# Attention tiles, bias and carry taken and released head by head; a pair's units by head; the gate's projection first and v's last; the last super-block's v by TensorE

## The chip, the cores and the metric

One core of a Trainium2 chip. TensorE (PE, with its weight loads PEld) multiplies, VectorE (DVE), ScalarE (ACT) and GpSimd (POOL) work on tiles, SyncE (SP) issues nearly all DMAs. The metric is the device time of the program in microseconds. Before the change it is 1274.22, the median of three runs (1273.27 to 1274.51).

## The reference

One layer over 2048 prompt frames and 64 frames of a running stream (sample). The input projection has eight parts of 512 columns: q, k, v and gate of attention, and q, f, i and gate of the recurrence.

```python
aq, ak, av, ag, hq, hf, hi, hg = jnp.split(rms_norm(x, ln_g) @ w_in, SPLITS, axis=-1)
o_a = attn_fn(heads(aq), k, v).reshape(B, T, W_A) * jax.nn.silu(ag)
o_b, S = hgrn2_branch(hq, hf, hi, hg, lb, norm_g, s0)
y = x + jnp.concatenate([o_a, o_b], axis=-1) @ w_out
```

Attention has 8 heads of 64; a chunk of 64 frames attends to itself and the 8 chunks before, with a learned bias by distance. The recurrence has 4 heads of 128. Results are y after a last RMSNorm, the k and v rows of the last 512 prompt frames and of the sample, and the recurrence's states. All is float32; the kernel splits each operand in a high and a low part (xh, xl; w's two halves) and adds three products.

## The kernel before

The tokens are cut in four super-blocks of 512 (the second, super-block 1, has the 64 sample frames too: 576, in two blocks of 256 and 320). In each, 32 projection jobs run: four groups of eight, the hgrn jobs hf, hq, hi, hg of one head and the attention jobs pv, pq, pk, pg of one pair of heads. A job is 24 matmuls of one block into an accumulator (acc, two buffers), and an eviction: `ev_q`, `ev_k`, `ev_v`, `ev_g`. The first two and the last two jobs of a super-block run by halves of 256 tokens, in turn. The list JOBS gives the order; in the last super-block its end is written out by hand.

The order on all engines is written by a planner (`Plan`). Each activity is a generator; it yields a time or a condition, and is resumed on the planner's own clock. Tokens (`Tok`) stand for buffers: vT (3 buffers for evicted q, k, v, i), sig (2), tr (2 PSUM banks for transposes), pv, s_ps (one score buffer), ph (2), pr (4), mixa (2), sga (2, the gate of a pair), kv (the tiles kd, v and q of one pair), bias. On the chip each engine then runs its instructions in this order and waits for semaphores.

A pair opens when the kv token is free, that is when the pair before has ended its last PV unit: `open_` loads the carried k and v of the 512 tokens before (L713, L714) and the bias (L674). q, k and v wait in vT buffers till then. `ev_q` copies q of both heads into the tile (ACT L732) and makes the low part and the swapped half (DVE L736, L737). `ev_k` does the same for k (L749 from the accumulator, L756, L760); rows that leave the kernel are turned by 32x32 blocks on DVE (L771) and written by four DMAs (L777). `ev_v` must put tokens on partitions: it turns blocks on DVE (L632), writes them to DRAM in four DMAs (way, L652), reads them back (L656), and then splits them (ACT L620, DVE L624); rows that leave are written at L612. hi, the input of the recurrence, goes the same way (copy at L1211).

The attention of a pair has four units, (first 256 queries, head 0), (first, head 1), (second, head 0), (second, head 1); `softmax_rows` makes the scores of 128 queries (s, L858 adds the bias and finds the minimum, L875 exp, L879 scales), `p_group` transposes the probabilities (tr, L887, L890), `attend` multiplies with v (pv) and adds the parts (mixa, L925, L929). After head 1 of a unit's queries the gate is multiplied in (L1027) and the result goes to DRAM (mixd, L1032). `sample_a` does the sample's attention in super-block 1.

After the last job comes the output projection, seven products for each of eight token groups (`out_step`): rows come from mixd into slots (L1619), weights from wod (L1961) into tiles that have become free: w, b11, xh and xl, then kd, q and ql when the last scores are done, and ph and v after the last PV. Projection weights of super-blocks 1 to 3 come from wd (L437). All DMAs named here are issued by SP in one order.

All matmuls are recorded at L249 (the helper `mm`), all transposes at L253.

Of the kernel before, what the change touches and what calls it, by code (L numbers as in the profile page):

```python
# [8 lines left out]
F32 = mybir.dt.float32  # L9
# [37 lines left out]
JOBS = [[(k, g) for g in range(4) for k in ("hf", "hq", "hi", "hg", "pv", "pq", "pk", "pg")] for _ in SUPER]  # L47
# [136 lines left out]
def hymba_step(  # L184
# [67 lines left out]
    def transpose(out, x, idn):  # L252
# [4 lines left out]
                                     w=WBUFS, raw=RAWB, xn=XNB, kv=1, q=1, rec=1, sga=2, bias=1, gf=1, gi=1, gg=1,  # L257
# [349 lines left out]
    def rows_out(src, out, row, nt, cols, t):  # L607

        rows = src.shape[0]
        s4 = src.rearrange("p (a t j) -> p t a j", a=4, t=nt)  # L610
        for i in range(nt):
            sp.dma_start(out[row + i * P : row + i * P + rows, cols].rearrange("p (a j) -> p a j", a=4), s4[:, i])  # L612
        return C.dma(nt * rows)

    def split_rows(src, v, t0, nt, rows, t):
        s = src.rearrange("p (h a t j) -> p h a t j", h=2, a=2, t=nt)
        hi = v[:rows, t0 : t0 + nt, 0::3, :].rearrange("p t h (a j) -> p h a t j", a=2)
        lo = v[:rows, t0 : t0 + nt, 1:3, :].rearrange("p t h (a j) -> p h a t j", a=2)
        for h in range(2):
            act.copy(hi[:, h], s[:, h])  # L620
        t = C.act(nt * P + 150, t)
        yield "D", t
        for h in range(2):
            dve.tensor_sub(lo[:, h], s[:, h], f32(hi[:, h]))  # L624
        return C.dve(nt * P + 60, t)
# [44 lines left out]
    def load_bias(sb, p, d):  # L670
        yield from tk["bias"].get()
        nb = d.bias = T(wk, [P, 2, 640], F32, "bias", bufs=1)
# [16 lines left out]
        d.bias_at = t  # L689
        yield t  # L690
        sp.dma_start(biasd[p], nb)
        C.dma(655)

    def pair_jobs(sb, p):
# [6 lines left out]
        d.q_n = d.k_n = d.v_n = 0  # L701
        d.q_t = d.k_t = d.v_t = 0.0
        d.bias_at = d.cache = None

        def open_():

            yield from tk["kv"].get()
            d.kd = T(pa, [P, 2, WIN + NMAX], F32R, "kd")
            d.v = T(pa, [P, 9, 4, 64], F32R, "v")
            d.q = T(pa, [P, 2, QW], F32R, "q")  # L710
            if sb:
                cd = carry[sb - 1][p]
                sp.dma_start(f32(d.kd[:, :, 0:512]), cd[:, 0:2, :])  # L713
                sp.dma_start(f32(d.v[:, 0:4].rearrange("p t s d -> p (t s d)")),  # L714
                             cd[:, 2:4, :].rearrange("p a c -> p (a c)"))
                d.k_t = d.v_t = C.dma(1024)
            C.spawn(load_bias(sb, p, d), 1)
            if smp:
                C.spawn(sample_cache(d), 1)

        def ev_q(acc, off, bn, t):
# [7 lines left out]
            yield lambda: d.q is not None  # L729
            yield "A", t  # L730
# [3 lines left out]
            yield "D", t - 600.0  # L734
            for h in range(2):
                dve.tensor_sub(ql[own[h], h, c], st[own[h], :bn], f32(d.q[own[h], h, c]))  # L736
                dve.tensor_copy(d.q[own[1 - h], h, c], f32(d.q[own[h], h, c]))  # L737
                t = C.dve(1.8 * bn, t)
                if h == 0:
                    yield "D", t - 300.0  # L740
            tk["vT"].put(1, t)
            d.q_n += bn
            d.q_t = max(d.q_t, t)

        def ev_k(acc, off, bn, t):
# [6 lines left out]
            yield lambda: d.kd is not None  # L752
            yield "A", t
            c = slice(512 + off, 512 + off + bn)
            for h in range(2):
                act.copy(d.kd[own[h], h, c], kn[own[h], :bn])  # L756
                t = C.act(bn, t)
            yield "D", t - 600.0
            for h in range(2):
                dve.tensor_sub(d.kd[own[1 - h], h, c], kn[own[h], :bn], f32(d.kd[own[h], h, c]))  # L760
                t = C.dve(1.2 * bn, t)
            d.k_n += bn
            d.k_t = max(d.k_t, t)
            full = bn // P * P
            for c, w, out in ((0, full, nk_prompt if last else None), (full, bn - full, nk_sample)):
                if not w or out is None:
                    continue
                yield from tk["sig"].get()
                yield "D", t
                st = T(wk, [P, 512], F32, "sig", bufs=2)  # L770
                dve.transpose(st[:, :w], kn[:, c : c + w])  # L771
                t = C.dve(w, t)
                yield t
                row = 0 if c else off
                to = out[row : row + w, p * P : (p + 1) * P].rearrange("(n i) (a j) -> a i n j", i=32, a=4)
                for a in range(4):
                    sp.dma_start(to[a], st[32 * a : 32 * a + 32, :w].rearrange("p (n j) -> p n j", j=32))  # L777
                tk["sig"].put(1, C.dma(w))
            tk["vT"].put(1, t)
            yield from got_all(True)  # L780

        def ev_v(acc, off, bn, t):
# [6 lines left out]
            yield lambda: d.v is not None  # L789
            yield "A", t  # L790
            full = bn // P * P
            for c, w, rows, out in ((0, full, P, nv_prompt if last else None),
                                    (full, P if bn > full else 0, bn - full, nv_sample)):
                if not w:
                    continue
                t = yield from split_rows(vt[:rows, c : c + w], d.v, 4 + (off + c) // P, w // P, rows, t)
                if out is not None:
                    t = rows_out(vt[:rows, c : c + w], out, 0 if c else off, w // P, slice(p * P, (p + 1) * P), t)
            tk["vT"].put(1, t)
            d.v_n += bn  # L800
            d.v_t = max(d.v_t, C.now + 1000.0)
            yield from got_all(False)

        def got_all(k):
            if last and p == NPAIR - 1 and d.v_n == d.k_n == d.q_n == n:
                have.add("projected")
            if not last and (d.k_n if k else d.v_n) == n:
                yield (d.k_t if k else d.v_t) + 500.0
# [3 lines left out]
                else:  # L812
                    sp.dma_start(cd[:, 2:4, :].rearrange("p a c -> p (a c)"),
                                 f32(d.v[:, 4:8].rearrange("p t s d -> p (t s d)")))
# [18 lines left out]
        C.spawn(open_(), 1)  # L833
# [6 lines left out]
        return d, dict(g=ev_g, q=ev_q, k=ev_k, v=ev_v)  # L840

    def softmax_rows(d, h, qc, spans, bcol, nk, out):

        yield lambda: d.q_n >= qc + P and d.k_n >= qc + P and d.bias_at is not None
        yield max(d.q_t, d.k_t, d.bias_at) + 300.0
# [18 lines left out]
        d.left -= 1  # L864
        if d.left == 0:
            if d.sb == len(SUPER) - 1 and d.p == NPAIR - 1:
                have.add("scores")
                tk["x4"].put()
            tk["bias"].put()
# [13 lines left out]
    def vcols(v, t, h, rows):  # L883
        return v[:rows, t, 2 * h : 2 * h + 2, :].rearrange("p s d -> p (s d)")
# [48 lines left out]
    def attend(d, g0, h, prs, mixes, before, mine):  # L933
# [39 lines left out]
        yield lambda: d.v_n >= g0 + 256  # L973
        yield d.v_t
# [21 lines left out]

    def attention(d):
# [4 lines left out]
        units = [(g0, h) for g0 in range(0, npr, 256) for h in range(2)]  # L1002
        d.left = 2 * len(units) + (1 if npr < n else 0)
# [13 lines left out]
        for i, ((g0, h), prs) in enumerate(zip(units, allprs)):  # L1017
            C.spawn(attend(d, g0, h, prs, mixes, marks[i - 1] if i else None, marks[i]), 1)
# [48 lines left out]
    def sample_a(d, c0, marks):  # L1067
        yield lambda: d.left == 1
        yield lambda: d.cache is not None and d.q_n >= c0 + DEC and d.k_n >= c0 + DEC and d.v_n >= c0 + DEC
        yield "D", max(d.q_t, d.k_t, d.v_t)  # L1070
# [35 lines left out]
        d.left -= 1  # L1106
        if d.left == 0:
            tk["bias"].put()
# [413 lines left out]
    def residual():  # L1522

        rooms = (("xn",), ("bias",), ("x4", "pr", "pr"), ("x5", "sga"))
# [320 lines left out]
    def program():  # L1845
# [4 lines left out]
        vroom = f32(T(pa, [P, 9, 4, 64], F32R, "v")).rearrange("p t s d -> p (t s d)")  # L1850
# [6 lines left out]
        for tag, n in (("raw", 2), ("xn", 3), ("kv", 1)):  # L1857
# [20 lines left out]
        def first_x():  # L1878
# [13 lines left out]
            tk["kv"].put()  # L1892
# [132 lines left out]
    def out_rows_a():  # L2025
# [6 lines left out]
        yield from tk["kv"].get()  # L2032
        lo = T(pa, [P, 9, 4, 64], F32R, "v").rearrange("p t s d -> p (t s d)")[:, : 4 * 512]
# [66 lines left out]
```

## Time and profile before

| | |
|---|---|
| median of the runs | 1274.22 us |
| the profiled execution | 1271.79 us, span 1270.1 us |
| granted TensorE clock, mean | 0.992 |
| TensorE busy | 1242.3 us |
| VectorE, ScalarE, GpSimd busy | 904.9, 681.3, 411.0 us |
| moved by DMA | 290.04 MB, 228 GB/s |

The span runs from the first to the last instruction of the profiled execution; the program's time is 1.7 us longer. Matmuls overlap in their pipeline, so the length of one row is more than what it adds; from the start of one row to the start of the next is what counts.

### The profile page before, as it was taken

Reading aid. Unit: us, or ns where it says so; the run is one execution under the profiler, and the core shown is the slowest. Engines: PE = TensorE matmul, PEld = TensorE weight load, DVE = VectorE, ACT = ScalarE, POOL = GpSimd, SP = SyncE. Lnnn points to the kernel's source line nnn. Section 1 sums busy time; section 2 is a strip of 40 time slices with the busy share of each in tenths; the row PEclk is TensorE's granted clock in tenths of the full one; section 3 lists DMA queues with packets and bytes.
Section 4 is the critical chain, followed back from the end, with each engine's and each line's share of the span. In section 5 each row is a group of like instructions: output and inputs, shape, how many; then the busy total and the mean of one; then the engine's idle time right before and its main releaser. Section 6 shows DMA issues by size and latency. Waiting matters only on the chain.

```text
span 1270.1 us, 21324 instructions
## 1 busy us (share of the span) xinstructions
PE 1242.3 (98%) x7482; PEld 1092.3 (86%) x7482; DVE 904.9 (71%) x1883; ACT 681.3 (54%) x1531; POOL 411.0 (32%) x700
## 2 busy tenths in 40 slices
PE   8999999999999999999999999999999998999997
PEld 7887888999999989988888888988888887878776
DVE  6688979766857667686575767776757666766775
ACT  5353636755647457574555555765546454643443
POOL 5656565111110111101242341034242204464543
PEclk9999999999999999999999999999999998999999
DMA  8887798657355484545968686667787577886431
GB/s 331 301 300 235 289 312 332 238 180 243 116 178 181 131 269 166 166 167 179 322 195 312 223 290 232 241 216 261 248 267 235 197 237 232 309 299 182 133 125 67
DMA packets 147893, 290.04 MB, mean 228 GB/s; under 512 B 50825, under 2 KB 93065, under 8 KB 130122
## 3 DMA queue, kind: packets, MB, share of 16 engines
q1 hardware_dynamic: 147496, 288.67, 67.5%
q8 instruction: 59, 0.97, 0.3%
q14 instruction: 48, 0.39, 0.1%
q10 hardware_dynamic: 290, 0.01, 0.0%
HBM read 196.36 MB, written 93.32 MB: 228 GB/s over the span
## 4 chain that ended last, share of the span: by engine, by line
PE 83%; DVE 5%; DMA 3%; issue 2%; POOL 2%; ACT 2%; SPq 1%; POOLq 0%; DVEq 0%; ACTq 0%
PE acc L249 59%; PE g L249 7%; PE tr L253 5%; PE s L249 5%; PE pv L249 5%; DMA vT<-way 2%; PE g L253 1%; PE g L1895 1%; DMA v<-wod 1%; DMA w<-wd 1%; POOL sig L1645 0%; SPq L1049 0%; DMA mixd<-ob 0%; POOL pr L1720 0%; POOL bias L1720 0%
## 5 line engine op out<-in xcount | busy, mean ns | idle before, releaser
L249 PE MATMUL acc<-xh,w 128*128 128x512 f32 (+2 forms) x2752 | 561.9, 345 | 7.2 <-ACT vT L749 6.4
L249 PEld LDWEIGHTS acc<-xh,w 128*128 128x128 f32 x2752 | 440.7, 190 | 57.6 <-ACT vT L749 7.1
L249 PE MATMUL acc<-xl,w 128*128 128x512 f32 (+2 forms) x1376 | 293.4, 346 | 0.3 <-DVE xl L407 0.3
L249 PEld LDWEIGHTS acc<-xl,w 128*128 128x128 f32 x1376 | 221.8, 190 | 25.3 <-DVE xl L407 0.5
L887 ACT CAST ph<-tr 128x512 fp32r<-128x512 f32 (+3 forms) x176 | 87.9, 507 | 102.1 <-PE pv L249 53.7
L858 DVE CUSTOM_DVE_ANT_0 pr<-s,bias 128x640 f32<-128x640 f32 (+4 forms) x128 | 94.1, 735 | 42.6 <-PE s L249 41.8
L464 POOL TENSOR_TENSOR w<-wraw,w 128x256 fp32r<-128x256 f32 x120 | 101.7, 875 | 61.2 <-DVE w L459 36.3
L875 ACT ACTIVATE pr<-pr,nm 128x640 f32<-128x640 f32 (+4 forms) x132 | 100.3, 760 | 34.8 <-DVE nm L858 32.6
L890 DVE TENSOR_TENSOR ph<-tr,ph 128x512 fp32r<-128x512 f32 (+3 forms) x176 | 100.8, 587 | 23.3 <-ACT ph L887 22.5
L249 PE MATMUL pv<-ph,v 128*128 128x256 f32 (+2 forms) x344 | 97.8, 371 | 0.8 <-DVE mixa L929 0.8
L1464 POOL TENSOR_TENSOR k<-ob 128x512 f32<-128x512 f32 (+2 forms) x20 | 18.7, 937 | 223.8 <-ACT ob L1455 200.6
L1027 POOL TENSOR_TENSOR mixa<-mixa,sga 128x256 f32<-128x256 f32 (+1 forms) x36 | 28.0, 778 | 195.0 <-DVE mixa L929 186.9
L253 PE MATMUL tr<-ident,pr 128*128 128x128 f32 x580 | 88.9, 275 | 1.2 <-DVE ph L890 0.9
L500 POOL TENSOR_TENSOR xn<-wraw,xn 128x256 fp32r<-128x256 f32 x48 | 38.2, 798 | 151.9 <-ACT xn L497 151.9
L929 DVE TENSOR_TENSOR mixa<-mixa,pv 64x256 f32<-64x256 f32 (+1 forms) x144 | 56.8, 394 | 40.9 <-ACT mixa L925 37.6
L879 DVE TENSOR_SCALAR pr<-pr,sm 128x640 f32<-128x640 f32 (+4 forms) x132 | 77.5, 587 | 4.7
L253 PEld LDWEIGHTS tr<-ident,pr 128*128 128x128 f32 x580 | 70.5, 142 | 11.7 <-DVE ph L890 2.0
L564 ACT ACTIVATE sig<-acc 128x256 f32<-128x256 f32 (+1 forms) x66 | 32.3, 489 | 79.2 <-PE acc L249 78.1
L249 PEld LDWEIGHTS pv<-ph,v 128*128 128x128 f32 (+1 forms) x344 | 58.0, 189 | 7.6 <-issue 0.9
L925 ACT COPY mixa<-pv 64x256 f32<-64x256 f32 (+1 forms) x72 | 25.1, 348 | 64.8 <-PE pv L249 56.3
L249 PE MATMUL s<-kd,q 128*128 128x320 f32 (+3 forms) x232 | 55.9, 311 | 1.6 <-DVE nm L858 1.6
L249 PE MATMUL s<-kd,ql 128*128 128x320 f32 (+3 forms) x232 | 55.6, 309 | 0.0
(320 smaller groups left out, 2137.3 us busy)
## 6 DMA issues: line engine op xcount, KB each, us to landing
w<-wd SPq DMA_DIRECT2D x96, 1024.0 KB, 6.0
wd<-w SPq DMA_DIRECT2D x32, 1024.0 KB, 7.0
wraw<-in_w_in_dram SPq DMA_DIRECT2D x30, 512.0 KB, 5.4
wod<-xn SPq DMA_DIRECT2D x28, 512.0 KB, 5.2
xn<-in_x_prompt_dram SPq DMA_DIRECT2D x23, 512.0 KB, 5.9
bias<-biasd SPq DMA_DIRECT2D x12, 640.0 KB, 8.3
way<-vT SPq DMA_DIRECT2D x96, 64.0 KB, 4.5
vT<-way SPq DMA_DIRECT2D x24, 256.0 KB, 4.0
```

The costliest lines, as they stand in the source:

```text
L249: pe.matmul(out, w, x, **kw)
L253: pe.transpose(out, x, idn)
L464: pool.tensor_sub(w[:, 1, k : k + 2], raw[:, k : k + 2], f32(w[:, 0, k : k + 2]))
L500: pool.tensor_sub(f32r(st[:, c.start + 512 : c.stop + 512]), src[:, c], st[:, c])
L564: act.activation(sig[:, :bn], acc, AF.Exp, scale=-1.0)
L858: dve.tensor_tensor_reduce(s[:, :nk].rearrange("p (a c) -> p a c", a=ns), sps[:, :ns, :kn], d.bias[:, h, bcol : bcol + nk].rearrange("p (a ...
L875: act.activation(s[:, :nk], s[:, :nk], AF.Exp, bias=nm[:, 0:1], scale=-1.0, accum_out=sm)
L879: dve.tensor_scalar(s[:, :nk], s[:, :nk], sm, None, ALU.mult)
L887: act.copy(ph[:krows, 0, :wid], pt[:krows, :wid])
L890: dve.tensor_sub(ph[:krows, 1, :wid], pt[:krows, :wid], f32(ph[:krows, 0, :wid]))
L929: dve.tensor_add(mix[hs, :qn], mix[hs, :qn], pv[hs, i, :qn])
L1027: pool.tensor_mul(mix[:, :n], mix[:, :n], d.sg[:, g0 : g0 + n])
```

## The change

Tokens and counters become one for each head: kv0 and kv1, bias0 and bias1, and lists of two for what has arrived. The tiles kd, v, q and bias are allocated once and stay (`room`); v is laid out by heads. `open_(h)` loads the carry of one head in two DMAs, and its bias in one. Units are ordered (first, head 0), (second, head 0), (first, head 1), (second, head 1), and kv0 is released after the second. A pair's jobs run pg, pq, pk, pv; the hand-written end of the last super-block keeps its own order. In the last super-block v's rows are made by TensorE transposes, four of 64 columns for each head, and the k and v rows that leave the kernel by transposes of 128x128, with one DMA for each block; the sample's k rows too.

```diff
-JOBS = [[(k, g) for g in range(4) for k in ("hf", "hq", "hi", "hg", "pv", "pq", "pk", "pg")] for _ in SUPER]
+JOBS = [[(k, g) for g in range(4) for k in ("hf", "hq", "hi", "hg", "pg", "pq", "pk", "pv")] for _ in SUPER]
 JOBS[-1][-12:] = [("hf", 3), ("hq", 3), ("pv", 2), ("pq", 2), ("pk", 2), ("hi", 3), ("hg", 3), ("pg", 2), ("pv", 3),
                   ("pq", 3), ("pk", 3), ("pg", 3)]
...
+    def new_rows(src, off, bn, p, out_p, out_s, tok, t):
...
+        yield from tk["tr"].get()
+        yield t
+        pt = tr_ps()
+        for a, b, rows, out in segs:
+            for j in range(a, b):
+                transpose(pt[:rows, j * P : (j + 1) * P], src[:, j * P : j * P + rows], ident)
+        t = C.pe()
+        tok.put(1, t)
+        for a, b, rows, out in segs:
+            s3 = pt[:rows, a * P : b * P].rearrange("p (t d) -> p t d", d=P)
+            yield from tk["sig"].get()
+            yield "D", t
+            st = T(wk, [P, 512], F32, "sig", bufs=2).rearrange("p (t d) -> p t d", d=P)
+            dve.tensor_copy(st[:rows, : b - a], s3)
...
         if sb:
-            sp.dma_start(nb, biasd[p])
-            d.bias_at = C.dma(655)
+            sp.dma_start(nb[:, h], biasd[p][:, h])
+            d.bias_at[h] = C.dma(330)
+            return
...
-        def open_():
-
-            yield from tk["kv"].get()
+        def open_(h):
+
+            yield from tk[f"kv{h}"].get()
...
             if sb:
                 cd = carry[sb - 1][p]
-                sp.dma_start(f32(d.kd[:, :, 0:512]), cd[:, 0:2, :])
...
+                sp.dma_start(f32(d.kd[:, h, 0:512]), cd[:, h])
+                d.k_t[h] = C.dma(256)
+                sp.dma_start(f32(d.v[:, h, 0:4].rearrange("p t s d -> p (t s d)")), cd[:, 2 + h])
+                d.v_t[h] = C.dma(256)
+            d.open[h] = True
+            C.spawn(load_bias(sb, p, d, h), 1)
...
+        def ev_v_last(acc, off, bn, t):
+            yield from tk["vT"].get()
+            yield "A", t
+            vt = T(wk, [P, 512], F32, "vT", bufs=VTB)
+            act.copy(vt[:, :bn], acc)
...
+            for h in range(2):
+                yield lambda: d.open[h]
+                yield from tk["tr"].get()
+                yield t
+                pt = tr_ps()
+                for j in range(nt):
+                    transpose(pt[:, j * 64 : j * 64 + 64], vt[own[h], j * P : (j + 1) * P], ident[own[h], own[h]])
+                yield "A", C.pe()
...
+                act.copy(hi, s3)
...
+                dve.tensor_sub(lo, s3, f32(hi))
...
+            yield from new_rows(vt, off, bn, p, nv_prompt, None, tk["vT"], t)
...
-        return d, dict(g=ev_g, q=ev_q, k=ev_k, v=ev_v)
+        return d, dict(g=ev_g, q=ev_q, k=ev_k, v=ev_v_last if last else ev_v)
...
-        yield lambda: d.v_n >= g0 + 256
-        yield d.v_t
+        yield lambda: d.v_n[h] >= g0 + 256
+        yield d.v_t[h]
...
-        units = [(g0, h) for g0 in range(0, npr, 256) for h in range(2)]
+        units = [(g0, h) for h in range(2) for g0 in range(0, npr, 256)]
...
-        yield lambda: all(m["end"] for m in marks)
-        tk["kv"].put(1, C.pe())
+        for h in range(2):
+            yield lambda: all(m["end"] for m, u in zip(marks, units) if u[1] <= h)
+            tk[f"kv{h}"].put(1, C.pe())
```

In ev_q, ev_k and ev_v the copies into the tiles wait for `d.open[h]` and run head by head.

TensorE where pair 3 of the last super-block opens, before: the last half of the gate's projection (acc_12711), the first product of the output projection (acc_12746, weights b11), and behind it the first scores of pair 3.

```order
L249 MATMUL acc_12711<-xl_154,w_12277 128x256 x8
L249 MATMUL acc_12711<-xh_153,w_12277 128x256 x8
L249 MATMUL acc_12746<-b11h_12620,slot_12624 128x512 x2
L249 MATMUL acc_12746<-b11l_12621,slot_12624 128x512
L249 MATMUL acc_12746<-b11h_12620,slot_12624 128x512 x2
L249 MATMUL acc_12746<-b11l_12621,slot_12624 128x512
L249 MATMUL acc_12746<-b11h_12620,slot_12624 128x512 x2
L249 MATMUL acc_12746<-b11l_12621,slot_12624 128x512
L249 MATMUL acc_12746<-b11h_12620,slot_12624 128x512 x2
L249 MATMUL acc_12746<-b11l_12621,slot_12624 128x512
L249 MATMUL s_12769<-kd_12655,q_12657 128x320 x2
L249 MATMUL s_12769<-kd_12655,ql_155 128x320 x2
```

The same place now: v of head 1 is transposed (vT_12496), k's second half is projected (acc_12679), with scores and the rows that leave the kernel between its matmuls.

```order
L253 MATMUL tr_12659<-ident_69,vT_12496 128x64 x4
L249 MATMUL acc_12627<-xh_153,w_12369 128x256 x8
L249 MATMUL acc_12679<-xh_153,w_12255 128x256 x2
L249 MATMUL s_12683<-kd_588,q_590 128x320 x2
L249 MATMUL s_12683<-kd_588,ql_155 128x320 x2
L249 MATMUL acc_12679<-xh_153,w_12255 128x256 x6
L249 MATMUL acc_12679<-xl_154,w_12255 128x256 x2
L253 MATMUL tr_12706<-ident_69,vT_12496 128x128 x4
L253 MATMUL tr_12711<-ident_69,vT_12633 128x128 x2
L249 MATMUL acc_12679<-xl_154,w_12255 128x256 x6
L249 MATMUL s_12727<-kd_588,q_590 128x320 x2
L249 MATMUL s_12727<-kd_588,ql_155 128x320 x2
```

The scores have moved from behind the first output product into k's second half. The second place is the first PV of pair 2 in super-block 1, on TensorE. Before, it stands in the second block of the gate's projection (acc_6001), the pair's last job, three jobs after v's.

```order
L249 MATMUL acc_5929<-xh_153,w_5552 128x256 x6
L249 MATMUL acc_6001<-xh_153,w_5552 128x320 x6
L253 MATMUL tr_6017<-ident_69,pr_5805 128x128
L253 MATMUL tr_6017<-ident_69,pr_5873 128x128
L249 MATMUL pv_5954<-ph_5968,v_5574 128x512 x2
```

Now v's job is the pair's last, and the first PV stands in the next job, the following hgrn head's hf (acc_5936, acc_5990).

```order
L249 MATMUL acc_5936<-xh_153,w_5546 128x256 x2
L249 MATMUL acc_5990<-xh_153,w_5546 128x320 x2
L249 MATMUL s_5997<-kd_588,q_590 128x320 x2
L249 MATMUL s_5997<-kd_588,ql_155 128x320 x2
L253 MATMUL tr_6007<-ident_69,pr_5871 128x128
L253 MATMUL tr_6007<-ident_69,pr_5905 128x128
L253 MATMUL tr_6007<-ident_69,pr_5871 128x128
L253 MATMUL tr_6007<-ident_69,pr_5905 128x128
L249 MATMUL acc_5990<-xh_153,w_5546 128x320 x4
L249 MATMUL pv_6026<-ph_5926,v_589 128x512 x2
```

The first PV keeps its place among the pair's scores, and v's job has come up to one job ahead of it.

More of the change, by code (lines that the diff above doesn't have):

```diff
@@ L605, in split_v, with rows_out @@
         return C.dve(nt * P, t)
-    def rows_out(src, out, row, nt, cols, t):
+    def rows_out(src, out, cols, t):
         rows = src.shape[0]
[L610 to L621, printed above, removed]
+        sp.dma_start(out[:rows, cols].rearrange("p (a j) -> p a j", a=4), src.rearrange("p (a j) -> p a j", a=4))
+        return C.dma(rows)
@@ L622, in split_rows @@
+    def split_rows(src, v, h, t0, nt, rows, t):
+        s = src.rearrange("p (h a t j) -> p h a t j", h=2, a=2, t=nt)[:, h]
+        hi, lo = (v[:rows, h, t0 : t0 + nt, x, :].rearrange("p t (a j) -> p a t j", a=2) for x in (h, 1 - h))
+        act.copy(hi, s)
+        t = C.act(nt * 64 + 80, t)
         yield "D", t
-        for h in range(2):
-            dve.tensor_sub(lo[:, h], s[:, h], f32(hi[:, h]))
-        return C.dve(nt * P + 60, t)
+        dve.tensor_sub(lo, s, f32(hi))
+        return C.dve(nt * 64 + 30, t)
@@ L761, in ev_k @@
                 t = C.dve(1.2 * bn, t)
[L762 to L768, printed above, removed]
-                yield "D", t
[L770 to L778, printed above, removed]
@@ L1105, in sample_a @@
         tk["s_ps"].put(1, t)
-        d.left -= 1
-        if d.left == 0:
-            tk["bias"].put()
+        for h in range(2):
+            d.left[h] -= 1
+            tk[f"bias{h}"].put()
         yield "A", t
```

168 lines of the change are left out of this document (102 added, 66 removed).

## The prediction

> **What bounds the kernel now.** I read the page first: its header, the busy times and the shares of the chain that ended last.
>
> ```profile
> span 1270.1 us, 21324 instructions
> PE 1242.3 (98%) x7482; PEld 1092.3 (86%) x7482; DVE 904.9 (71%) x1883; ACT 681.3 (54%) x1531; POOL 411.0 (32%) x700
> PE 83%; DVE 5%; DMA 3%; issue 2%; POOL 2%; ACT 2%; SPq 1%; POOLq 0%; DVEq 0%; ACTq 0%
> ```
>
> TensorE is busy for 98% of the span. So a change can gain only TensorE's gaps (1270.1 - 1242.3 = 27.8 us) and whatever slows it down, and any matmul added is paid in full. Next I read the waits of TensorE: total, times, longest.
>
> ```profile
> PE acc L249 <- ACT vT L749: 6.4, 2, 5.4
> PE g L249 <- ACT k L1406: 2.0, 1, 2.0
> PE acc L249 <- DMA v<-wod: 1.8, 1, 1.8
> PE s L249 <- DVE nm L858: 1.6, 2, 1.2
> PE acc L249 <- DMA ph<-wod: 1.4, 1, 1.4
> ```
>
> Four of the five lie in the last super-block, where pair 3 is opened and the output weights follow. The table by stretches shows that they cost more than their length: its columns are stretch, length, busy TensorE (x matmuls), granted clock, DMA share, GB/s.
>
> ```profile
> 1064.00:1073.20 9.20, 3.78 (x32) 0.88 0.90 327
> 1073.20:1081.00 7.80, 7.79 (x37) 0.70 0.76 213
> 1081.00:1092.00 11.00, 9.38 (x43) 0.84 1.06 330
> 1128.80:1140.00 11.20, 8.08 (x28) 0.85 0.87 322
> ```
>
> After the gap at 1067 to 1073 the granted clock is 0.70 for 7.8 us, and around the two smaller places 0.84 and 0.85. A stall is paid twice, as a gap and as slow matmuls behind it.
>
> **Transposes added.** The order of TensorE gains 68 instructions: 32 transposes of 128x128 (k and v rows of the last super-block), 32 of 128x64 (v by heads), 4 of the sample's k. The prices come from the timeline (start, length, engine; what counts is from start to start), the last row from the transposes' line:
>
> ```profile
> 888.93 0.46 PE L249 MATMUL s<-kd,ql 128*128 128x320 f32 x2
> 889.23 0.62 PE L249 MATMUL acc<-xl,w 128*128 128x512 f32 x2
> 889.69 1.04 PE L253 MATMUL tr<-ident,pr 128*128 128x128 f32 x8
> 890.48 1.42 PE L249 MATMUL acc<-xl,w 128*128 128x512 f32 x5
> ...
> 1064.03 1.83 PE L249 MATMUL acc<-xh,w 128*128 128x256 f32 x14
> 1065.70 1.12 PE L249 MATMUL acc<-xl,w 128*128 128x256 f32 x8
> ...
> L253 PE MATMUL tr<-ident,xn x76: 222/272/280, 14.2 to 819.3; 128*128 128x128 f32 x72, 64*128 64x64 f32 x4
> ```
>
> Eight transposes take 890.48 - 889.69 = 0.79 us, 0.099 each; a matmul of 512 columns takes 0.23, of 320 0.15, of 256 0.12. The shortest of the last row, 50 ns below the median, are those with 64 columns, so a narrow one costs about half. 36 x 0.099 + 32 x 0.05 = 5.2 us; with no discount 68 x 0.099 = 6.7. Nothing hides it. I take **+5.2**, bounds 5.2 and 6.7. The evictions that come with them (8 casts on ACT, 8 subtractions and 13 copies on DVE) replace the same number of splits and 9 block transposes, on engines 54% and 71% busy: 0.
>
> **Opening of pair 3.** The chain of waits, and TensorE's row that ends it:
>
> ```profile
> 1058.41 5.37 DMA mixd<-ob
> 1063.85 1.14 ACT slot L1619 x2
> 1066.33 1.51 DVE v L624 x2
> ...
> 1071.58 1.13 DVE ql L736
> 1072.79 0.38 ACT vT L749
> 1073.21 2.07 PE L249 MATMUL acc<-xh,w 128*128 128x256 f32 x8 [5.43 <-ACT vT L749]
> ```
>
> Pair 2 holds q, k and v to its last PV matmul (at 1063.8). Only then do v, q and k of pair 3 go into the tiles, both heads in one line on DVE (1066.33 to 1072.7); the second half of k waits for a vT buffer that q still holds, its accumulator stays full and TensorE stops. It costs 5.43 us of gap and 7.80 x (1 - 0.70) = 2.3 us of slow clock, 7.7 in all. After the change head 0's tiles come free when pair 2's head 0 has ended, two units earlier, so half of that line is done before; and the buffer that k's second half takes was v's, whose last reader is now a transpose five rows ahead on TensorE. What is late next is head 1's share, about half of those 6 us on DVE. Between the last PV and the stop 30 matmuls of 256 columns stood (3.6 us); now 46 stand there with 8 of scores and 10 transposes, 5.5 + 1.2 + 0.8 = 7.5 us. I leave 1.3 us: **-6.4**, bounds -7.7 (gone) and 0 (all stays).
>
> **Scores between too little work.**
>
> ```profile
> 1085.52 0.56 PE L249 MATMUL s<-kd,q 128*128 128x320 f32 x2 [0.46 <-DVE nm L858]
> 1087.52 0.56 PE L249 MATMUL s<-kd,q 128*128 128x320 f32 x2 [1.16 <-DVE nm L858]
> ```
>
> Pair 3's scores start late and stand close together, each waiting for DVE to empty the one score buffer. Gap 0.46 + 1.16 = 1.6, clock 9.38 x (1 - 0.84) = 1.5. Now the first two stand inside k's second half and the third behind the gate's (the second piece of order above). I take half: **-1.6**, bounds -3.1 and 0.
>
> The page "TensorE: Matmul & The Clock Gate" of the Trainium skill (Part 1: The HAM clock gate) says that the clock drops after an idle window of about 3.4 us. This trace agrees for the 5.43 us gap, but gaps of 0.46 and 1.16 us, and below of 1.36 and 1.76, stand beside 0.84 and 0.85 as well. By the rule these two places would cost their gaps alone, and the sum would be -2.7 rather than -4.6.
>
> **Output weights behind the last PV.**
>
> ```profile
> 1123.49 0.40 PE L249 MATMUL pv<-ph,v 128*128 128x256 f32 x2
> 1124.87 0.90 SPq L1961 DMA_DIRECT2D v<-wod  x2
> 1130.27 0.70 PE L249 MATMUL acc<-ph,slot 128*128 128x512 f32 x2 [1.36 <-DMA ph<-wod]
> 1132.74 0.80 PE L249 MATMUL acc<-v,slot 128*128 128x512 f32 x1 [1.76 <-DMA v<-wod]
> ```
>
> The weights of the last product are loaded over ph and v, after the last PV. It takes 1132.7 - 1123.7 = 9.0 us from that PV to the landing. Before, 22 matmuls of 512 columns stood between (0.23 each: 5.1 us). After, 46 stand between, 10.6 us. Cost now: 1.36 + 1.76 = 3.1 of gap and 8.08 x (1 - 0.85) = 1.2 of clock. Margin is 1.6 us: **-4.0**, bounds -4.3 and 0.
>
> **v last in a pair.** In super-blocks 0 to 2 v still goes to DRAM and back, and the first PV is now behind it, where k's and the gate's jobs stood in between (30 us of matmuls or more in super-block 1). This is a new wait: TensorE takes its instructions in order, so behind a PV that waits stand the projections. The nearest slack is in super-block 1, pair 2. From the end of v's first half to the first PV the order has 30 matmuls of 320 columns, 24 of 256, 12 of scores, 8 in the recurrence and 15 transposes: 30 x 0.15 + 24 x 0.12 + 12 x 0.15 + 1.4 + 1.5 = 12.1 us. Pairs 0 and 1 have 12.7 and 14.6 counted so, all others 14.9 or more. The trip itself, from the turn on DVE to the cast on ACT, in the hgrn part (gi) and in v:
>
> ```profile
> 417.35 0.45 DVE L632 STREAM_TRANSPOSE vT<-acc 128x256 f32<-128x256 f32 x1 [0.58 <-PE acc L249]
> 429.76 0.42 ACT L1211 COPY gi<-vT 128x256 f32<-128x256 f32 x1
> 438.61 0.45 DVE L632 STREAM_TRANSPOSE vT<-acc 128x256 f32<-128x256 f32 x1
> 458.50 0.50 ACT L620 CAST v<-vT 128x128 fp32r<-128x128 f32 x2 [4.05 <-DMA vT<-way]
> ```
>
> 12.4 us in one case, 19.9 in the other. The second shared SP with the opening of a pair:
>
> ```profile
> 449.15 0.98 SPq L713 DMA_DIRECT2D kd<-carry  x1
> ...
> 454.05 2.69 SPq L656 DMA_DIRECT2D vT<-way  x1
> ```
>
> With the gate's job first the opening is issued three jobs ahead of v, so I take the first, 12.4, plus 1.1 for cast and subtraction of one head: 13.5 against 12.1, 12.7 and 14.6. The shortage is 1.4 + 0.8: **+2.2**, bounds 0 and +24 (19.9 + 1.1 against each of the three: 8.9 + 8.3 + 6.4 = 23.6).
>
> **The rest at 0.** An opening now issues six DMAs for three, 12 times, 0.5 to 1 us of SP each as in the row of kd<-carry above (up to 3 us an opening); against it the last super-block loses small ones. SP's total goes from 761 to 748. In super-block 1 the openings issue both heads together in the new order, so head by head gives nothing there; if that cover were gone, it would show as a late weight load, which no row has today. Taking the gate first claims one of two sga buffers three jobs earlier; the pair that held it ended a pair before. The one 2.0 us wait for k at L1406 lies in a stretch that is reordered; I count it neither way, +-3.
>
> **Sum.** 5.2 - 6.4 - 1.6 - 4.0 + 2.2 = -4.6 us. The profiled execution took 1271.8 us, so 1267.2 for it; it lies 2.4 below the median of the runs, 1274.2, which puts the median at **1269.6 us** (-0.36%). Within 0.2%, 2.5 us, this kernel's runs can't be told from no change.
>
> **Rivals.**
> - **v comes too late (slower).** In super-block 1 the trip stays long, since its SP queue still holds k's carry, the sample's state and the rows of the sample between way and back. At 16 us, with 1.1 for cast and subtraction, the shortage is 5.0 + 4.4 + 2.5 = 11.9 for 2.2: net +5.1, 1279.3. Clock loss behind three stalls would add to it, and at 19.9 us it is about 1291. It decides from about 15 us. For it: the row of 19.9. Against it: the rows of the hgrn trips, the same path without an opening beside it.
> - **The opening stays (same).** ACT still stands at the first slot cast until mixd<-ob has landed (1058.41 to 1063.8), and head 1's splits still follow it on DVE. With -1 in place of -6.4 and 0 for the scores: 5.2 - 1 - 4.0 + 2.2 = +2.4, 1276.6. Against it: k's second half no longer takes q's buffer.
> - **Gains of the end eaten in the middle (same).** Trips of 13.3 to 15 us cost 4 to 9 in place of 2.2: net -2.5 to +2.3, 1271.7 to 1276.5, about 1274 in the middle. For it: several waits of ACT for these trips are in the trace (4.05 us in the row above), so they often land later than the order has them.
>
> **How the numbers follow.** Forecast 0.52, v too late 0.20, the opening stays 0.13, eaten 0.15. The forecast's own range is 1264 to 1272, so a little of it lies within 0.2%; faster 0.50, same 0.28, slower 0.22. The low end: all four terms at their best give 5.2 - 7.7 - 3.1 - 4.3 = -9.9, 1264.3, and 1263 with part of the reordered wait. The high end, 1280, takes in the 16 us case.
>
> **What would show it.** In the profile after: TensorE's wait for vT at L749's successor under 1.5 us and a clock near 1.0 where pair 3 opens; no wait for ph or v from wod; tr<-ident,vT at 0.1 us a piece from start to start; waits of PV for v (DVE) under 3 us in all. The prediction is wrong if TensorE waits for v's subtraction in super-blocks 0 to 2 for more than 7 us, or if the gap at pair 3 only moves to another buffer.

## The result, and the profile after

The changed kernel takes 1258.22 us (median; 1256.82 to 1259.63), the kernel before beside it 1274.37 us (1273.27 to 1276.05). The ratio is 0.9872, with an interval of 0.9854 to 0.989: 1.3% faster, where 0.36% was forecast. 1258.2 lies below the low end of the range, 1263. The page after, header, busy times and the shares of the last chain by engine:

```profile
span 1254.6 us, 21417 instructions
PE 1240.9 (99%) x7550; PEld 1093.7 (87%) x7550; DVE 894.6 (71%) x1887; ACT 684.7 (55%) x1533; POOL 415.2 (33%) x700
PE 5%; DVE 2%; POOL 2%; DMA 2%; issue 2%; ACT 1%; POOLq 0%; DVEq 0%; ACTq 0%; SPq 0%
```

TensorE runs 68 instructions more and yet is busy 1.4 us less: it ran at a fuller clock (0.996 in the mean, 0.992 before). (The chain ends in another place and was followed back a shorter way; its shares do not compare.) The longest waits of TensorE, in total, times, longest:

```profile
PE g L1953 <- POOL one L279: 1.4, 1, 1.4
PE g L253 <- DVE xn L377: 1.0, 1, 1.0
PE tr L253 <- DVE kd L377: 0.9, 1, 0.9
PE acc L249 <- DVE pr L1772: 0.6, 1, 0.6
```

All five waits that the prediction began with are gone; what leads the list now stands at the start of the program, of a super-block and in the output projection. The stretches at the end, in the columns of the prediction's table:

```profile
1055.00:1070.00 15.00, 15.00 (x119) 14.46 (x118) 11.26 (x23) 8.48 (x19) 8.90 (x12) 1.00 0.90 337
1070.00:1085.00 15.00, 14.43 (x84) 12.35 (x83) 9.85 (x25) 8.85 (x21) 2.70 (x4) 1.00 0.85 300
1085.00:1100.00 15.00, 14.74 (x75) 12.11 (x74) 13.79 (x30) 10.66 (x25) 13.57 (x17) 1.00 0.97 379
1100.00:1115.00 15.00, 15.00 (x74) 12.48 (x73) 7.26 (x14) 4.77 (x10) 12.21 (x19) 1.00 0.83 291
1115.00:1130.00 15.00, 14.75 (x65) 11.87 (x64) 12.44 (x15) 9.82 (x26) 8.96 (x9) 1.00 0.91 264
```

(Behind TensorE's busy time stand those of its weight loads, VectorE, ScalarE and GpSimd.) The clock is 1.00 in all five, where it was 0.70, 0.84 and 0.85. The product with the last weights (ph and v), which stood at 1130 before, now runs in the last of them, from 1117.95 on, and waits for neither. TensorE's rows where pair 3 opens:

```profile
1061.77 0.46 PE L253 MATMUL tr<-ident,vT 64*128 64x64 f32 x4
1062.16 1.45 PE L249 MATMUL acc<-xh,w 128*128 128x256 f32 x10
...
1065.00 0.82 PE L253 MATMUL tr<-ident,vT 128*128 128x128 f32 x6
1065.57 0.95 PE L249 MATMUL acc<-xl,w 128*128 128x256 f32 x6
```

No gap is left. Four narrow transposes take 1062.16 - 1061.77 = 0.39 us, six wide ones 0.57: 0.098 and 0.095 each.

The two profiled executions differ in one place that the change has nothing to do with: four matmuls at the start took 3.78 us in the one and 1.98 in the other, with the same order around them. About 2.3 us of the 15.5 between the spans is this; the changed kernel profiled again started as the kernel before had.

```profile
5.13 3.78 PE L1906 MATMUL s<-gin,ones 1*128 1x512 f32 x4
```
```profile
4.89 1.98 PE L1964 MATMUL s<-gin,ones 1*128 1x512 f32 x4
```

**Where the time went.** For the following table each distance from one matmul's start to the next one's was taken from the records, less the usual distance (lower quartile) of that form in the changed kernel. What is left, summed by stage in us, is time lost to gaps and slow clock. Each row of the table is one profiled execution. A stage is counted in jobs of 24 x 512 columns; super-blocks end at 32, 68, 100 and 132, so 66-76 is the seam behind super-block 1, and 76-108 holds the one behind super-block 2 (a seam is the passage from one super-block to the next). H is heads (tokens, carry, bias, units), J the order of jobs, T the transposes in place of v's trip and VectorE's block transposes.

| kernel | 0-32 | 32-66 | 66-76 | 76-108 | 108-124 | 124-end | all | ratio to before (interval) |
|---|---|---|---|---|---|---|---|---|
| before | 14.1 | 16.6 | 5.5 | 5.1 | 2.4 | 21.4 | 65.1 | 1 |
| J | 13.4 | 12.2 | 16.6 | 11.8 | 3.2 | 16.3 | 73.5 | 1.0023 (1.0004-1.0042) |
| T | 13.3 | 16.1 | 11.6 | 6.1 | 5.7 | 18.1 | 70.9 | 1.0064 (1.0039-1.0089) |
| H | 13.5 | 25.2 | 6.8 | 5.1 | 2.6 | 18.2 | 71.4 | 1.0036 (1.0013-1.0059) |
| JT | 13.2 | 12.8 | 10.2 | 10.6 | 10.9 | 20.3 | 77.9 | 1.0096 (1.0071-1.0122) |
| HT | 13.3 | 25.1 | 6.7 | 5.4 | 4.0 | 10.3 | 64.8 | 1.0013 (0.9991-1.0035) |
| HJ | 8.9 | 12.5 | 3.3 | 4.8 | 3.4 | 12.8 | 45.8 | 0.9856 (0.9832-0.9879) |
| HJT (the change) | 9.8 | 14.2 | 3.5 | 4.9 | 4.7 | 7.1 | 44.2 | 0.9872 (0.9854-0.989) |

The end lost 14.3 us less, the first three super-blocks 8.9 less (2.3 of them the start), the rest of the last super-block 2.3 more.

Two cautions go with the table. Counted in the same way, the changed kernel profiled again differs from its row by 2.8 us in the first stage, which holds the start, and by at most 0.6 in the others; HJ profiled again loses 5.7 us more in all, up to 2.1 in one stage. And T, which in the first three super-blocks changes only how the sample's k rows leave, loses 6.1 us more at the first seam. So a new order by the planner can move losses of that size by itself, and a stage without a named wait shows no cause.

### The profile page after: what moved, and what is told of

It is laid out like the page before. It is cut to its first block, busy times and chain, and to the rows that moved or that the text cites. A ratio compares the mean times of both kernels' runs of the same rounds, so it can differ in the third digit from the quotient of the medians.

```text
span 1254.6 us, 21417 instructions
## 1 busy us (share of the span) xinstructions
PE 1240.9 (99%) x7550; PEld 1093.7 (87%) x7550; DVE 894.6 (71%) x1887; ACT 684.7 (55%) x1533; POOL 415.2 (33%) x700
## 5 line engine op out<-in xcount | busy, mean ns | idle before, releaser
L249 PEld LDWEIGHTS acc<-xl,w 128*128 128x128 f32 x1376 | 220.2, 189 | 25.1 <-DVE xl L407 0.5
L464 POOL TENSOR_TENSOR w<-wraw,w 128x256 fp32r<-128x256 f32 x120 | 106.6, 914 | 56.9 <-DVE w L459 40.4
L253 PEld LDWEIGHTS tr<-ident,pr 128*128 128x128 f32 x580 | 69.9, 140 | 10.8 <-DVE sig L634 1.0
L1521 POOL TENSOR_TENSOR k<-ob 128x512 f32<-128x512 f32 (+2 forms) x20 | 18.2, 911 | 180.7 <-ACT ob L1512 161.9
L564 ACT ACTIVATE sig<-acc 128x512 f32<-128x512 f32 (+2 forms) x64 | 32.0, 499 | 64.8 <-PE acc L249 61.7
L978 ACT COPY mixa<-pv 64x256 f32<-64x256 f32 (+1 forms) x72 | 25.1, 349 | 62.3 <-PE pv L249 58.7
L249 PE MATMUL s<-kd,q 128*128 128x320 f32 (+2 forms) x232 | 56.5, 314 | 0.0
L249 PE MATMUL s<-kd,ql 128*128 128x320 f32 (+2 forms) x232 | 55.7, 310 | 0.0
```

The source lines that it names most:

```text
L249: pe.matmul(out, w, x, **kw)
L253: pe.transpose(out, x, idn)
L464: pool.tensor_sub(w[:, 1, k : k + 2], raw[:, k : k + 2], f32(w[:, 0, k : k + 2]))
L564: act.activation(sig[:, :bn], acc, AF.Exp, scale=-1.0)
```

## The experiments

**The parts apart.** J alone, on the kernel before:

```diff
-... ("hf", "hq", "hi", "hg", "pv", "pq", "pk", "pg")] for _ in SUPER]
+... ("hf", "hq", "hi", "hg", "pg", "pq", "pk", "pv")] for _ in SUPER]
```

> The kernel before with the job order alone changed (gate, q, k, v). Theory (the small gaps of TensorE between 100 and 570 us, 8.6 us in all, went by the order of the jobs, and the end went by the heads): the gaps of the middle fall by about 6 us, the three gaps of the end stay (5.6, 1.9 and 3.8 us), 1274.4 - 5.5 = about 1269. Rival (the middle went because tiles come free head by head): the gaps of the middle stay and v's trip is a new wait, 1274 to 1280.

1276.82 against 1272.62 us: a time of the rival, but neither mechanism as it was set. Super-block 1 lost 4.4 us less: the theory's part, and there ScalarE's waits for v's trip fell from 18.0 to 1.2 us. But the seams lost 18 us more. SyncE, ScalarE and TensorE at the first of them:

```profile
540.60 4.54 SPq L777 DMA_DIRECT2D out_dram<-sig x4
545.24 0.39 SPq L811 DMA_DIRECT2D carry<-kd x1
545.73 5.67 SPq L652 DMA_DIRECT2D way<-vT  x8
```
```profile
556.80 0.50 ACT L620 CAST v<-vT 128x128 fp32r<-128x128 f32 x2 [4.78 <-DMA vT<-way]
```
```profile
559.23 0.80 PE L249 MATMUL g<-asb,gi 128*128 128x128 f32 x2 [4.24 <-DVE So L1425]
```

v's first block was turned at 534.84, and its four DMAs went out at 537.52. Its way back was issued only at 551.92, behind k's four DMAs (4.54 us) and the eight of v's second block (5.67 us). The copy of v holds up ScalarE until 556.8, 22.0 us after the turn. The state So that TensorE waits for was loaded behind the same DMAs. At the end the gap is still there, only with another releaser:

```profile
PE acc L249 <- DVE sga L569: 6.6, 1, 6.6
```

T alone, on the kernel before: `ev_v_last` and `new_rows` as in the change, with one token.

> The kernel before with TensorE's transposes alone: v of the last super-block, and the k and v rows that leave the kernel; one token for both heads, old order of jobs and units. Theory (the opening waits for the last PV of pair 2, whatever makes v): 68 transposes cost 6.4 us, the gap at the opening of pair 3 stays above 4 us, 1274.4 + 6 = about 1280. Rival (the opening went because v no longer holds a buffer through its trip): the gap falls under 1 us with its slow clock, 1274.4 + 6.4 - 7.7 = about 1273.

1280.59 us: the theory's time (8.0 us more, for 6), but not its sign. At the opening of pair 3 TensorE now waits 2.25, 1.09 and 0.26 us, 3.6 together where the theory had more than 4, the longest for VectorE's subtraction of v (L821); the clock over 1081 to 1092 us is 0.69. So the transposes without the heads break up the stop and do not remove it. By stage the end lost 3 us less, the seam 6 more.

H alone: the changed kernel with the old JOBS, `v=ev_v` in all super-blocks and VectorE's block transposes for k.

> Tokens, carry, bias and units head by head alone; old order of jobs, v through DRAM and rows by VectorE in the last super-block as before. Theory (the heads removed the stops of the end): opening 7.7, scores 3.1, output weights 4.3 go, 1274.4 - 15 = about 1259.5, the gaps of the middle stay at 8 us or so. Rival (the end needs v by TensorE): the gap at the opening of pair 3 stays at 4 us or more, only the output weights go, 1270.

1277.45 us: a miss. TensorE's wait at the opening of pair 3 is gone, as expected, but other waits stand in the last super-block (for mixa 2.8 us, for sm 2.1), and super-block 1 lost 8.6 us more. Its costliest place, ScalarE and TensorE:

```profile
382.77 0.62 ACT L601 CAST wraw<-ck 128x512 fp32r<-128x512 f32 x1 [3.86 <-DMA ck<-in_cache_attn_v_dram]
...
388.85 0.30 ACT L651 CAST v<-vT 128x128 fp32r<-128x128 f32 x1 [4.46 <-DMA vT<-way]
389.06 0.37 ACT L785 COPY vT<-acc 128x256 f32<-128x256 f32 x1
...
389.47 2.08 PE L249 MATMUL acc<-xh,w 128*128 128x256 f32 x8 [4.75 <-ACT vT L785]
```

The copy of v stands on ScalarE ahead of k's eviction (L785). It waits 4.46 us for the trip; k's accumulator stays full, TensorE stops 4.75 us. SyncE shows where the trip spent its time: behind the first block's four DMAs it issued the opening's four loads and two biases, then the second block's eight DMAs in 7.3 us, and only then the first way back:

```profile
366.03 2.50 SPq L682 DMA_DIRECT2D way<-vT  x4
368.57 0.43 SPq L752 DMA_DIRECT2D kd<-carry  x1
...
370.48 0.91 SPq L708 DMA_DIRECT2D bias<-biasd  x2
...
372.43 7.30 SPq L682 DMA_DIRECT2D way<-vT  x8
...
380.26 0.50 SPq L686 DMA_DIRECT2D vT<-way  x1
```

That is 14.2 us on the queue. In the kernel before the same stretch is not shorter (360.83 to 377.57), but there the copy followed 2.2 us behind the issue of the way back; here it follows 8.6 us behind. Why the way back landed so late was not followed up.

HJ: the changed kernel without T.

> The changed kernel without its transposes: v through DRAM and rows by VectorE in the last super-block, as before. Theory (the transposes are pure cost): all stops go as in the changed kernel, 6 us less of matmuls, 1258.2 - 6 = about 1252. Rival (v through DRAM arrives too late at the end): a wait of a PV or of an eviction for v of pair 3 of 5 us or more, 1258 to 1268.

1255.75 against 1272.62 us, between the theory's 1252 and the rival's 1258. J adds 0.2% without the heads and takes 1.8% with them (0.9856 to 1.0036): the gain belongs to the two together. ScalarE still waits 12.9 us for v's trip in this kernel, 11.1 of them in the last super-block, and yet it is the fastest: ScalarE's waits in sum do not tell what TensorE loses.

HT, the changed kernel with the old JOBS:

> The changed kernel with the old order of jobs in all super-blocks (v, q, k, gate); heads and transposes stay. Theory (v's copy stands on ScalarE ahead of k's eviction and waits for its trip, and only v's job behind q and k takes that away): ScalarE waits 15 us or more for v's trip, TensorE stops at k's eviction in super-block 1 for 5 us or more, about 1277 + 6 - what v by TensorE saves in the last super-block, 1272 to 1283. Rival (in the heads' run v through DRAM in the last super-block was the loss, not the order): 1260.

1274.9 us, as the theory has it for time and place (25.1 us lost in super-block 1); ScalarE's wait for v was 10.0 us, less than the 15 expected, and TensorE stopped 4.6 us at k's eviction for the 5 expected. JT, without the heads:

> The kernel before with the new order of jobs and the transposes, but one token for both heads and the old order of units. Theory (the order of jobs only pays when a pair can open by heads while the pair before still works): the opening of pair 3 stops TensorE for 4 us or more as with the jobs alone, and the openings of super-block 1 too, 1276.8 + 6 = about 1280. Rival (jobs and v by TensorE are enough): 1260 to 1266.

1286.01 us: slower than the theory's 1280, and not by its mechanism: its wait at the opening of pair 3 is 1.6 us. What grew are the seams and waits for the softmax on VectorE (L905, 7.8 us in seven waits).

**The two moves of the job order**, in the changed kernel. Gate first, v second, and then v behind k, gate last:

```diff
-... "pg", "pq", "pk", "pv")] for _ in SUPER]
+... "pg", "pv", "pq", "pk")] for _ in SUPER]
```

> The changed kernel with the gate first but v second (gate, v, q, k): one of the two moves of the job order. Theory (v's place behind k is what counts): ScalarE waits for v's trip as with the old order, 10 us or more in all, and the gaps of super-block 1 come back: 1266 to 1278. Rival (the gate's job ahead of all gives the opening its time, and v's place does not matter): within 2 us of the changed kernel, 1256 to 1260.

1272.56 us (0.9985, 0.9969 to 1.0001): the theory. Super-block 1 lost 21.2 us for 14.2, about half of what this kernel loses against the changed one, and ScalarE waits for the trip again:

```profile
ACT v L649 <- DMA vT<-way: 10.2, 5, 5.2
```

TensorE's longest stop there, 2.7 us, is not at k's eviction but for the state So, whose update on VectorE stands behind v's subtraction and then waits 0.9 us for its own load.

```diff
-... "pg", "pq", "pk", "pv")] for _ in SUPER]
+... "pq", "pk", "pv", "pg")] for _ in SUPER]
```

> The changed kernel with q, k, v, gate: v behind k, the gate last. Theory (v behind k is what counts): ScalarE's wait for v's trip stays under 8 us, q and k now wait for the opening in the vT buffers, a few small gaps: 1257 to 1264. Rival (the gate first is what counts): the evictions of q and k wait for vT, gaps of 8 us or more: 1268 or more.

1282.89 us (1.009, 1.0063 to 1.0117): slow as in the rival, by another wait. ScalarE waits for v only 2.9 us, as in the theory; but now TensorE waits for the accumulator of a gate to be emptied:

```profile
PE acc L249 <- DVE sga L569: 7.2, 2, 3.9
```

So neither move keeps the time of the two together. How the gate's waits come about was not followed up: one (3.3 us) stands where super-block 1 ends, the other (3.9) at the opening of pair 3, where the jobs are written out by hand and the gate stands as in the changed kernel.

**The order of units**, in the changed kernel, put back:

```diff
-        units = [(g0, h) for h in range(2) for g0 in range(0, npr, 256)]
+        units = [(g0, h) for g0 in range(0, npr, 256) for h in range(2)]
```

> The changed kernel with the old order of units (first half head 0, first half head 1, second half head 0, second half head 1): tokens, carry and bias still by heads. Theory (head 0's tiles come free only one unit before head 1's, so the opening loses most of its lead): the gap at the opening of pair 3 comes back with 3 to 5 us and its slow clock, 1258 + 6 = about 1264. Rival (the order of the jobs gives the opening its time): no gap over 1 us there, 1256 to 1260.

1262.78 us (0.9918, 0.9897 to 0.9938): a time between the two, the trace of the rival. No gap over 1 us stands at the end, so the theory's mechanism is refuted. By stage it loses 3 us more in super-block 0 apart from the start's 2.3, and nothing to speak of elsewhere. The interval overlaps with that of the changed kernel measured again (0.9874 to 0.9908, below), so a price of the old order of units is not shown.

**Is it v's trip?** v by TensorE in all super-blocks, so that there is no trip to wait for (108 transposes more), in HT, JT and HJT:

```diff
-        return d, dict(g=ev_g, q=ev_q, k=ev_k, v=ev_v_last if last else ev_v)
+        return d, dict(g=ev_g, q=ev_q, k=ev_k, v=ev_v_last)
```

(`ev_v_last` also takes the sample's 64 rows and writes the carry.)

> Heads and transposes with the old order of jobs, and v by TensorE in all four super-blocks: no trip of v through DRAM anywhere, 108 transposes more (10.5 us). Theory (v's trip ahead of k's eviction is what the heads alone lose in super-block 1): the time lost by TensorE between jobs 32 and 66 falls from 25 us to 15 or less, the evictions of k no longer stop TensorE; 1274.9 + 10.5 - 10 = about 1275. Rival (the openings of the pairs come late there whatever brings v): the loss stays above 20 us, 1285.

1274.22 us, the theory. The loss between jobs 32 and 66 falls from 25.1 to 15.8 us, the single losses of more than 0.2 us in it from 10.3 to 0.7.

> New order of jobs and transposes with one token for both heads, and v by TensorE in all super-blocks. Theory (v's trip is late where a super-block ends): the time lost between jobs 66 and 76 and between 98 and 108 falls from 17 us together to 8 or less; 1286 + 10.5 - 10 = about 1286. Rival (a pair with one token opens too late behind the gate's job, and its softmax then meets the next super-block's norm on VectorE): the loss stays at 14 us or more, 1296.

1293.38 us: between the two. At the seams 9.0 + 2.6 = 11.6 us are lost for 17.3 (10.2 + 7.1). The seam behind super-block 2 was the trip (7.1 to 2.6); the one behind super-block 1 was not (10.2 to 9.0).

> The changed kernel with v by TensorE in all super-blocks. Theory (no trip is waited for any more in the changed kernel, so there is nothing to win): 108 transposes at 0.097 us are added in full, 1258.2 + 10.5 = about 1268.7, the losses by stage as in the changed kernel. Rival (evictions behind the trip still cost): 1260 to 1264.

1278.52 us: a miss upward. The 108 transposes add 11.4 us in the records, and losses come back in super-blocks 0 and 1 (3.0 us without the start, and 5.5, which hold a part of the transposes' own time). Where v's round trip is hidden, taking it away wins nothing.

**The price of the transposes.** v's rows for the output taken from the narrow transposes; k's rows by VectorE again; both:

```diff
+                dve.tensor_copy(st[:, :nt, h * 64 : h * 64 + 64], s3)
-            yield from new_rows(vt, off, bn, p, nv_prompt, None, tk["vT"], t)
```

> The changed kernel, where v's rows for the output are copied from the transposes that make v by heads, so 16 of the 128x128 transposes go. Theory (every transpose is paid in full on TensorE, 0.107 us each): 1258.2 - 1.7 = 1256.5. Rival (they stand in time that TensorE has to wait anyway): no change, 1258.

> The changed kernel with the k rows that leave turned by VectorE and written by four DMAs a block as before; v stays on TensorE. 20 transposes of 128x128 go. Theory (paid in full): 1258.2 - 2.1 = 1256. Rival (the small DMAs hold SP's queue and sig's buffers, and an eviction waits for them): 1258 to 1264.

> Both of these: v's rows from the transposes by heads, k's rows by VectorE; 36 transposes fewer, 32 narrow ones stay. Theory (paid in full): 1258.2 - 3.9 = 1254.3, the same as the kernel without any transposes within its interval (1255.75). Rival (k's small DMAs cost what the transposes save): 1256 to 1260.

1256.36 (0.9867), 1258.94 (0.9889) and 1260.2 us (0.9895), with intervals of 0.002 to either side: none can be told from the changed kernel or from one another, so they do not decide between theory and rival. The third has waits of 2.6 and 2.3 us at the end that the others have not. Last, the changed kernel and HJ on the same chip:

> The changed kernel itself, beside the one without transposes on the same chip. Both theories: 1256 to 1260, ratio 0.987.

> The changed kernel without its transposes, on the same chip as the changed one. Theory (the transposes are paid in full, but the last super-block and the end lose 4 us less with them): 1 to 3 us faster than the changed kernel, ratio about 0.9855. Rival (nothing is given back): 6 us faster, ratio 0.982.

1259.77 (0.9891, 0.9874 to 0.9908) and 1256.5 us (0.9859, 0.9838 to 0.988): 3.3 us for HJ, a little over the theory's 1 to 3, with intervals that still overlap. HJ has the lowest ratio in both of its measurements. By these two times about half of the 6.1 us that the transposes cost comes back. The table shows where: with the heads, v by TensorE lowers the loss from job 124 on from 18.2 to 10.3 us (H to HT) and from 12.8 to 7.1 (HJ to HJT), and in HJT the stages ahead of it lose 4.2 us more than in HJ.

## Why the prediction was wrong

The mechanisms at the end were right, and the sign: none of the prediction's signs of being wrong appeared. The size failed in three terms of the sum (transposes, the group of gains at the end, v last in a pair) and most in one that was set to nothing, "the rest at 0".

- **Transposes, +5.2: 6.1 measured.** 68 steps of 0.09. The step "a narrow one costs about half" failed: the 32 narrow ones took 3.1 us for 1.6, the 36 others 3.0 for 3.6. The duration of a row had been taken for its step, the time from its start to the next start.
- **Opening, -6.4, scores, -1.6, output weights, -4.0.** The opening went in full (7.7: no gap, clock 1.00). Of the scores' 3.1 us 2.5 went. The 0.57 us of gap between 1070 and 1085 is a new wait: transposes of probabilities wait for VectorE to copy out new rows (L634). The weights' 4.3 went. Together 14.5 for 12.0; by stage the end gives 14.3. Margins had been subtracted at each place. That the three are one chain, so that the two places behind an early opening come early too, fits this but was not tested by itself.
- **v last in a pair, +2.2: 0.** No PV waits for v. The work between was counted right (12.1 and 14.6 us; the trace has 12.2 and 14.8 from the turn to the PV), but the trip was priced by one row of the hgrn part, 12.4 us from turn to copy. VectorE's turn and subtraction, then the PV, in pair 2:

```profile
461.28 0.44 DVE L660 STREAM_TRANSPOSE vT<-acc 128x256 f32<-128x256 f32 x1
...
471.66 0.28 DVE L652 TENSOR_TENSOR v<-vT,v 128x128 fp32r<-128x128 f32 x1
...
473.45 0.86 PE L249 MATMUL pv<-ph,v 128*128 128x512 f32 x3
```

10.7 us from the turn to the end of the subtraction here, 10.8 and 13.3 in pairs 0 and 1, for 13.5 assumed. The 19.9 us of the other row was no property of the trip but of its place: from turn to copy the same pair now takes 9.3. (In the rival "gains of the end eaten in the middle" 4 to 9 us in place of 2.2 make -2.8 to +2.2, not -2.5 to +2.3.)

- **"The rest at 0", and v last once more: -6.6, of which 4.8 stand behind v's copy.** This is the larger error. The first three super-blocks lost 8.9 us less, 6.6 without the start. The prediction looked at v's move only for the wait that it could bring to TensorE, and not for the one that it takes from ScalarE. Its own row of 458.50 shows ScalarE standing 4.05 us ahead of k's eviction. Of such waits there are 18.5 us before, 18.0 of them in super-block 1, and behind two of them TensorE stops. The first place, where TensorE then waits 1.01 us for L749; the second, ScalarE and TensorE; and all such waits, before and after:

```profile
379.76 0.50 ACT L620 CAST v<-vT 128x128 fp32r<-128x128 f32 x2 [3.37 <-DMA vT<-way]
380.16 0.36 ACT L749 COPY vT<-acc 128x256 f32<-128x256 f32 x1
```
```profile
464.56 0.50 ACT L620 CAST v<-vT 128x128 fp32r<-128x128 f32 x2 [3.62 <-DMA vT<-way]
...
466.07 0.52 ACT L1406 COPY k<-g 128x256 f32<-128x256 f32 x2
```
```profile
466.64 1.75 PE L249 MATMUL g<-gi,k 128*128 128x128 f32 x6 [2.02 <-ACT k L1406]
```
```profile
ACT v L620 <- DMA vT<-way: 18.5, 8, 4.0
```
```profile
ACT v L649 <- DMA vT<-way: 1.8, 1, 1.8
```

The 2.02 us wait that was left "neither way" ends 2.1 us after ScalarE is released from v. Behind it the clock is 0.50 for 3.4 us (466.9 to 470.3), so it costs 2.02 + 1.7 = 3.7 us; that is what the four jobs around it lose less after the change, and those around the first place lose 1.1 less. J alone agrees: it takes ScalarE's waits in super-block 1 from 18.0 to 1.2 us and TensorE's loss there from 16.6 to 12.2. The rival "gains eaten in the middle" quoted ScalarE's waits as a sign against the change; here they were a part of the gain. The rest of the 6.6 stands where ScalarE waits for no v: about 2 us less in super-block 0 and 2 less at the first seam, and 2.6 more at the start of super-block 1. Its causes stay open.
- **Parts that cannot be added.** The sum took heads and job order as two terms. J without H costs 0.2%, H without J 0.4%, both together gain 1.4%. That v's trip is what H alone loses in super-block 1 is shown by taking the trip away (25.1 to 15.8 us); for J without the heads it is shown at the second seam only. What J loses at the first seam, and so a part of what the heads bring there, stays open, as does how much of each step is only the planner's new order.
- **The rule on the clock.** The Trainium skill ("TensorE: Matmul & The Clock Gate", Part 1: The HAM clock gate) speaks of an idle window of about 3.4 us before the clock drops. This case's traces differ, and they decide. Before, the clock was back at 1.00 from 1078 to 1088 us, and then 0.50 from 1088.2 to 1091.5, behind gaps of 0.46 and 1.16 us; and it was 0.50 from 466.9 to 470.3, behind a single gap of 2.02 us. With the gaps of 0.46 to 1.76 us gone, the clock at both places rose from 0.84 and 0.85 to 1.00, as the prediction had it. The sum by the rule, -2.7, was further off than the one taken.

## What to carry to other kernels

When a step with a long latency is moved, look at every in-order queue on which its result is copied: what stands behind that copy is freed, and that may be worth more than what the step's consumer risks (here 4.8 us against 0). Price a move of order and the release of buffers that it needs as one term, and test them as two by two. What a small instruction adds on TensorE is read from start to start.

## What was not expected of the hardware

A transpose of 64 columns took 0.098 us from start to start, one of 128 columns 0.095. A single gap of 2.02 us on TensorE was followed by 3.4 us at a clock of 0.50. Small DMAs weigh by their issue: eight on SyncE took 7.3 us in one place and 5.67 in another, and the way back of v stands behind them on that queue. From the turn to the copy v's trip took 8.5 us in one place (307.52 to 315.98 in the changed kernel) and 22.0 in another (J).
